# Six depthwise convolution tiles as pairs of positions on TensorE, put right by SBUF transfers

## The chip, the cores and the metric

The kernel runs on one core of a Trainium2 chip. The metric is the device time of one execution, in microseconds; smaller is better. Engines are named as the profile names them: PE is TensorE (PEld its weight loads), DVE is VectorE, ACT is ScalarE, POOL is GpSimd, SP is SyncE, which here only issues DMAs.

## What is computed

The whole trunk of a small diffusion backbone: four layers (RG-LRU, Conformer convolution, neighbourhood attention, RG-LRU), each followed by an MLP, for 128 context and 256 latent tokens of width 1024. The change lies in layer 1, the Conformer module:

```python
def _conformer_conv(h, w_pw1, b_pw1, dw_w, dw_b, ln_g, ln_b, w_pw2, b_pw2):
    val, gate = jnp.split(h @ w_pw1 + b_pw1, 2, axis=-1)
    z = val * jax.nn.sigmoid(gate)
    z = _dwconv_centred(z, dw_w, dw_b)        # 31 taps, each channel by itself
    z = jax.nn.silu(_layernorm(z, ln_g, ln_b))
    return z @ w_pw2 + b_pw2
```

Context and latent tokens are convolved apart, each with zeros beyond its ends. Everything is float32.

## The kernel before

Activations lie with 128 channels on the partitions and the 384 tokens along the free axis, so the 1024 channels are eight tiles, m = 0 to 7. `conformer` goes through them in an order written out by hand. Engines run their own instructions in that order (a scheduler moves some of them within what the data allow), and wait for one another on semaphores.

For each tile `pwin(m)` multiplies by the two column blocks of pw1 (the weights are loaded as `raw` chunks of 1 MB on SP, and split into a high and a low part, `whi` by ACT and `wlo` by DVE), and `glu` makes z from the two products: tanh and a scaled copy on ACT, one product on DVE. z is written into `zp`, a padded row of both token groups with 15 zeros between and around them.

The depthwise convolution is done in two ways. Tiles 0 and 1 (`conv_dve`) take one DVE instruction for each tap over 399 columns. Tiles 2 to 7 go to PE (`conv_mm`): 32 channels at four shifts are the 128 rows of a product, so one product covers four taps, eight steps cover all, and four column groups of 32 channels make up the tile. The rows for that, `z4`, are made by DMA: `zp` goes to DRAM (`zd`), and four DMAs read it back, each with its shift, into 32 partitions. All of these are issued on POOL. The weights `dg`, nearly diagonal blocks made on the host, are loaded on SP. There are three `z4` buffers, so tile m waits for the convolution of tile m-3.

The result of a convolution lies in PSUM with its channels in the right rows. ACT adds the bias for the four tiles in `FIRST`; these four make the mean of LayerNorm first (`shift`: a product with ones gives `mu`, which is taken off so that the sums of squares stay accurate); the later tiles subtract `mu` as they are read. Tile 7 comes last in two segments, the 256 latent columns and then the 128 context columns (`stats`), and is followed at once by the sums of LayerNorm, the normalization (`normed`) and pw2 (products named p). Columns of the modulation matrix for later layers (`pmwl`, products named pmp) are loaded ahead and multiplied behind tile 7.

On PE the order is pw1 of tiles 2 to 5, conv 2, conv 3, pw1 of tiles 6 and 7, conv 4, the mean, conv 5, conv 6, conv 7.

DMAs report their landing on eight semaphores for those issued on SP and ACT (DMAHW0 to 7) and on eight for those issued on POOL (DMASW0 to 7). They are counted off over these in program order; a DMA that shares a semaphore with an earlier one waits until that one has landed.

Of the kernel before, what the change touches and what calls it, by code (L numbers as in the profile page):

```python
# [7 lines left out]
F32 = mybir.dt.float32  # L8
# [3 lines left out]
ALU = mybir.AluOpType  # L12
# [15 lines left out]
CW = 31  # L28
CG = SEQ + 15 + LAT
CSEG = ((0, 0, SEQ), (1, SEQ + 15, CG))  # L30
CP = CG + CW
PE_CONV = (2, 3, 4, 5, 6, 7)
TAP = CW // 4 + 1
ZW = CG + 4 * (TAP - 1)

NH = 16
# [53 lines left out]
LNACT = (1, 3)  # L90
FIRST = (2, 3, 0, 4)
WARM0, WARM1, WARM2 = 20, 8, 4
# [24 lines left out]
@with_exitstack  # L117
def trunk(ctx, tc, wst, wmod, vecs, condr, xin, kcT, vcache, rpbt, diag, ident_in,
          y_out, st_out, k_out, v_out):
# [79 lines left out]
    MODS.clear()  # L199
    loaded = {}  # L200

    def load_chunk(i):
        if plan[i][0] == "gates":
            g = []
            for d in range(2):
                g.append(state["lp"].tile([P, 1024], F32, tag="graw", name=f"graw{i}{d}", bufs=3))
                nc.sync.dma_start(g[d], wst[i, :, d * 1024:d * 1024 + 1024])
            return g
        raw = wp.tile([P, 2048], F32, tag="raw", name=f"raw{i}", bufs=2)
        nc.sync.dma_start(raw, wst[i])  # L210
# [608 lines left out]
    def conformer(l, j, nrm):  # L819
        mv = need(l, G1)  # L820
        with (tc.tile_pool(name=f"cf{l}", bufs=1) as cp,
              tc.tile_pool(name=f"cd{l}", bufs=1, space=bass.MemoryType.DRAM) as dp):
            zps = [cp.tile([P, CP], F32, tag="zp", name=f"zp{l}{i}", bufs=KT) for i in range(KT)]
            for z in zps:
# [3 lines left out]
            def glu(m, pv, pg, c=None):  # L828
                th = tmp(f"gth{l}{m}")[:, :N]
                v = tmp(f"gv{l}{m}")[:, :N]  # L830
                if c is None:
                    nc.scalar.activation(th, pg[:, :N], AF.Tanh, scale=0.5, bias=hb1[:, KT + m:KT + m + 1])
                    nc.scalar.activation(v, pv[:, :N], AF.Identity, scale=0.5, bias=hb1[:, m:m + 1])
# [12 lines left out]
                if m in PE_CONV:  # L846
                    z4 = cp.tile([P, 4, ZW], F32, tag="z4", name=f"z4{l}{m}", bufs=3)
                    zd = dp.tile([P, CP], F32, tag="zd", name=f"zd{l}{m}", bufs=3)
                    nc.gpsimd.dma_start(zd, z)
                    zg = zd.rearrange("(g c) n -> c g n", g=4)  # L850
                    for s in range(4):
                        nc.gpsimd.dma_start(z4[32 * s:32 * s + 32], zg[:, :, s:s + ZW])
                    z4s[m] = z4
                    dgs[m] = wp.tile([P, D], F32, tag="dmw", name=f"dg{l}{m}", bufs=3).rearrange("p (t n) -> p t n", t=TAP)
                    nc.sync.dma_start(dgs[m], diag[PE_CONV.index(m)])

            z4s, dgs, convs = {}, {}, []

# [13 lines left out]

            def conv_pe(m):
                zcs[m] = zc = cp.tile([P, N], F32, name=f"zc{l}{m}")
                ps = conv_mm(m, f"cps{l}{m}", 0, CG)
                for s, a, e in CSEG:
                    _, xa, xb = SEG[s]
                    if m in first:
                        nc.scalar.activation(zc[:, xa:xb], ps[:, a:e], AF.Identity, bias=dwb[:, m:m + 1])
                    else:  # L880
                        nc.vector.scalar_tensor_tensor(zc[:, xa:xb], ps[:, a:e], dwb[:, m:m + 1], mu[:, xa:xb],
                                                       op0=ALU.add, op1=ALU.subtract)
                if m not in first:
                    moments(m)

            def conv_dve(m):
                zcs[m] = zc = cp.tile([P, N], F32, name=f"zc{l}{m}")
                t = cp.tile([P, CG], F32, tag="zt", name=f"zt{l}{m}", bufs=1)
                z = zps[m]
                nc.vector.tensor_scalar(t, z[:, 0:CG], dww[:, m, 0:1], dwb[:, m:m + 1],  # L890
                                        op0=ALU.mult, op1=ALU.add)
                for k in range(1, CW - 1):
                    nc.vector.scalar_tensor_tensor(t, z[:, k:k + CG], dww[:, m, k:k + 1], t,  # L893
                                                   op0=ALU.mult, op1=ALU.add)
                k = CW - 1
                for s, a, e in CSEG:
# [18 lines left out]
            def shift():  # L915
# [3 lines left out]
                for m in first:  # L919
                    center(m)  # L920

            keep = {}
            h = nrm.start([chunk("pw1", j, m) for m in range(2)], f"pw{l}0_",
# [26 lines left out]
            preload(AF.Abs_reciprocal_sqrt, zcs[6][:, 0:1])  # L950
            for i in range(LNPRE):
                t = None
                if i > 3:
                    t = cp.tile([P, 4, ZW], F32, tag="z4", name=f"pmwl{i}", bufs=3)
                    t = t.rearrange("p a b -> p (a b)")[:, :D]
                elif i > 1:
                    t = cp.tile([P, D], F32, tag="pm", name=f"pmwl{i}", bufs=2)
                ready[len(MODS) + i] = mod_load(len(MODS) + i, into=t)
            dl = cp.tile([P, N], F32, name=f"dl{l}")
# [283 lines left out]
def lay_out(i):  # L1243
    import numpy as np
    i = {k: np.asarray(v) for k, v in i.items()}
    chunks = []
    for key in weight_plan():
# [58 lines left out]
    vecs = np.concatenate([bm, cd, sel, lcw, cols(i["lru_conv_b"]), cols(i["lru_b_a"]), cols(i["lru_b_x"]),  # L1306
                           cols(i["lru_lambda"]), cols(i["state_lru"][0]),
                           cols(i["conf_b_pw1"][0].reshape(2, D)), dww, cols(i["conf_dw_b"][0]),
                           cols(i["conf_ln_g"][0]), cols(i["conf_ln_b"][0]), cols(i["conf_b_pw2"][0]),
                           cols(i["final_g"])], axis=1)  # L1310
# [15 lines left out]

    diag = np.zeros((len(PE_CONV), P, TAP, P), f4)
    w = i["conf_dw_w"][0]
    ch = np.arange(32)
    for n, m in enumerate(PE_CONV):  # L1330
        for t in range(TAP):
            for s in range(4):
                if 4 * t + s < CW:
                    for g in range(4):
                        diag[n, 32 * s + ch, t, 32 * g + ch] = w[4 * t + s, m * P + 32 * g + ch]
    ident = np.zeros((P, P), f4)
    ident[np.arange(P), np.arange(P)] = 1
    return dict(wst=wst, wmod=wmod, vecs=vecs, condr=condr, xin=xt, kcT=kcT, vcache=vc, rpbt=rpbt,
                diag=diag, ident_in=ident)

# [29 lines left out]
```

## Time and profile before

| what | value |
|---|---|
| median of 3 runs | 1757.38 us (1752.82 to 1760.23) |
| the profiled execution, its time | 1757.44 us |
| its span in the trace | 1755.7 us |
| TensorE busy | 1725.0 us, 98% |
| mean granted clock | 0.996 |
| the Conformer of layer 1, first product of pw1 to first of pw2 | 456.90 to 575.50 us |

The span runs from the first instruction to the last; the execution's own time is 1.7 us longer. The profile is of that one execution. Times in the trace are from the start of the span. The "chain" follows the work that ended last back to what released it, step by step. In rows of instructions, `out<-in` are the program's names, with the numbers of tiles left out in the profile: `cps` is the convolution's PSUM, `z` is z4, `pw` a product of pw1, `p` one of pw2. A float32 product has two records in the trace, so a tile's 32 products are 64.

### The profile page before, as it was taken

Reading aid. Unit: us, or ns where it says so; the run is one execution under the profiler, and the core shown is the slowest. Engines: PE = TensorE matmul, PEld = TensorE weight load, DVE = VectorE, ACT = ScalarE, POOL = GpSimd, SP = SyncE. Lnnn points to the kernel's source line nnn. Section 1 sums busy time; section 2 is a strip of 40 time slices with the busy share of each in tenths; the row PEclk is TensorE's granted clock in tenths of the full one; section 3 lists DMA queues with packets and bytes.
Section 4 is the critical chain, followed back from the end, with each engine's and each line's share of the span. In section 5 each row is a group of like instructions: output and inputs, shape, how many; then the busy total and the mean of one; then the engine's idle time right before and its main releaser. Section 6 shows DMA issues by size and latency. Waiting matters only on the chain.

```text
span 1755.7 us, 27298 instructions
## 1 busy us (share of the span) xinstructions
PE 1725.0 (98%) x10442; PEld 1626.0 (93%) x10442; DVE 1404.6 (80%) x2791; ACT 946.3 (54%) x1697; POOL 21.6 (1%) x46
## 2 busy tenths in 40 slices
PE   8999999999998999999999999999999999999997
PEld 7779999999985999999987889999999779999997
DVE  5998899999896989889785668889999978843443
ACT  4876662453633774255365657524546976733531
POOL 0000000000021000000000000000000000000000
PEclk9999999999999999999999999999999999999998
DMA  9665367776485247766554423667764413533331
GB/s 387 237 217 179 125 223 255 242 239 237 160 237 170 76 145 251 238 238 232 185 185 160 133 85 132 215 230 236 244 239 167 151 54 121 172 129 120 124 139 39
DMA packets 66996, 322.43 MB, mean 184 GB/s; under 512 B 7952, under 2 KB 12176, under 8 KB 43696
## 3 DMA queue, kind: packets, MB, share of 16 engines
q1 hardware_dynamic: 64944, 314.11, 52.2%
q0 software_dynamic: 1920, 6.57, 1.5%
q8 instruction: 82, 1.34, 0.3%
q14 instruction: 50, 0.41, 0.1%
HBM read 316.69 MB, written 3.96 MB: 183 GB/s over the span
## 4 chain that ended last, share of the span: by engine, by line
PE 77%; DVE 15%; ACT 4%; issue 2%; DMA 1%; SPq 0%; POOL 0%; DVEq 0%; ACTq 0%
PE f L129 29%; PE o L129 27%; PE pw L129 4%; PE lo L129 3%; DVE mjunk L329 3%; PE qk L129 3%; DVE wlo L217 2%; PE p L129 2%; PE wo L129 2%; PE v L129 2%; DVE xf L606 1%; PE cps L129 1%; PE s L129 1%; PE po L129 1%; DVE tr L648 1%
## 5 line engine op out<-in xcount | busy, mean ns | idle before, releaser
L216 ACT ACTIVATE whi<-raw 128x1024 fp32r<-128x1024 f32 x360 | 379.0, 1060 | 545.7 <-PE o L129 326.5
L217 DVE TENSOR_TENSOR wlo<-raw,whi 128x1024 fp32r<-128x1024 f32 x360 | 437.9, 1222 | 161.2 <-ACT whi L216 160.8
L329 DVE SCALAR_TENSOR_TENSOR mjunk<-dmw,condb 128x1024 bf16<-128x1024 f32 x308 | 375.7, 1220 | 1.5
L129 PE MATMUL o<-hl,whi 128*128 128x384 f32 x1024 | 343.0, 335 | 0.0
L129 PE MATMUL o<-hh,wlo 128*128 128x384 f32 x1024 | 343.0, 335 | 0.0
L129 PE MATMUL o<-hh,whi 128*128 128x384 f32 x1024 | 343.0, 335 | 0.0
L129 PEld LDWEIGHTS o<-hh,wlo 128*128 128x128 f32 x1024 | 192.2, 188 | 0.0
L129 PEld LDWEIGHTS o<-hh,whi 128*128 128x128 f32 x1024 | 192.2, 188 | 0.0
L129 PEld LDWEIGHTS o<-hl,whi 128*128 128x128 f32 x1024 | 192.2, 188 | 0.0
L499 DVE SCALAR_TENSOR_TENSOR x<-o,modv,x 128x128 f32<-128x128 f32 (+1 forms) x128 | 47.4, 413 | 68.2 <-PE o L129 68.2
L129 PE MATMUL g<-xf,graw 128*128 128x386 f32 x256 | 85.7, 490 | 1.8 <-DVE gl L664 1.8
L129 PEld LDWEIGHTS g<-xf,graw 128*128 128x128 f32 x256 | 47.9, 190 | 34.4 <-DVE gl L664 2.5
L783 DVE TENSOR_TENSOR hl<-s,hh 128x384 fp32r<-128x384 f32 x128 | 71.2, 556 | 7.4 <-ACT s L782 3.1
L781 ACT ACTIVATE hh<-r 128x384 fp32r<-128x384 f32 x128 | 67.2, 525 | 3.3
L782 ACT ACTIVATE s<-r 128x384 f32<-128x384 f32 x128 | 65.3, 511 | 0.0
L777 ACT ACTIVATE r<-f 128x384 f32<-128x384 f32 x112 | 52.9, 473 | 12.2 <-PE f L129 12.2
L129 PE MATMUL lo<-yh,wlo 128*128 128x384 f32 x128 | 43.5, 340 | 1.6 <-DVE wlo L217 1.6
L129 PE MATMUL lo<-yl,whi 128*128 128x384 f32 x128 | 43.0, 336 | 0.0
L129 PE MATMUL lo<-yh,whi 128*128 128x384 f32 x128 | 42.6, 336 | 0.0
L129 PE MATMUL cps<-z,dg 128*32 128x399 f32 (+2 forms) x448 | 34.7, 467 | 4.5 <-DMA z<-zd 4.5
L893 DVE SCALAR_TENSOR_TENSOR zt<-zp,vec,zt 128x399 f32<-128x399 f32 x58 | 36.7, 632 | 1.2
L129 PEld LDWEIGHTS cps<-z,dg 128*32 128x32 f32 x448 | 14.6, 114 | 23.8 <-issue 22.4
(1515 smaller groups left out, 4030.4 us busy)
## 6 DMA issues: line engine op xcount, KB each, us to landing
raw<-wst SPq DMA_DIRECT2D x180, 1024.0 KB, 5.0
dmw<-wmod SPq DMA_DIRECT2D x154, 512.0 KB, 4.1
pmw<-wmod SPq DMA_DIRECT2D x34, 512.0 KB, 7.3
graw<-wst SPq DMA_DIRECT2D x16, 512.0 KB, 5.1
bt<-rpbt SPq DMA_DIRECT2D x16, 384.0 KB, 3.3
z<-zd POOLq DMA_DIRECT2D x24, 213.5 KB, 6.3
dg<-diag SPq DMA_DIRECT2D x6, 512.0 KB, 4.8
pmwl<-wmod SPq DMA_DIRECT2D x4, 512.0 KB, 5.4
```

The costliest lines, as they stand in the source:

```text
L129: i = nc.tensor.matmul(*a, **kw)
L216: nc.scalar.activation(hi, raw[:, s], AF.Copy)
L217: nc.vector.tensor_tensor(lo, raw[:, s], hi.bitcast(F32), op=ALU.subtract)
L329: nc.vector.scalar_tensor_tensor(mjunk, w, 0.5, condb[:, s], op0=ALU.mult, op1=ALU.mult, accum_out=mod_tile(l)[:, c, m, s:s + 1]))
L499: nc.vector.scalar_tensor_tensor(x[m][:, xa:xb], ps[:, a:b], mv[:, g, m, s:s + 1], x[m][:, xa:xb], op0=ALU.mult, op1=ALU.add)
L606: nc.vector.scalar_tensor_tensor(xf, r[:, k:k + LG], lcw[:, j, t, k:k + 1], xf, op0=ALU.mult, op1=ALU.add)
L648: nc.vector.tensor_tensor_scan(tr[:, 2 + mt, ::-1], a[:, 2 + mt, ::-1], ti[:, 2 + mt, ::-1], h0v[:, j, 1, t:t + 1], op0=ALU.mult, op1=ALU.add)
L777: nc.scalar.activation(r, ps[:, :N], AF.Relu)
L781: nc.scalar.activation(hh, r, AF.Square)
L782: nc.scalar.activation(s, r, AF.Square)
L783: nc.vector.tensor_tensor(hl, s, hh.bitcast(F32), op=ALU.subtract)
L893: nc.vector.scalar_tensor_tensor(t, z[:, k:k + CG], dww[:, m, k:k + 1], t, op0=ALU.mult, op1=ALU.add)
```

## The change

- Tiles 1 to 6 are convolved by `conv_pair`. A product's 128 rows are 16 channels by 8 successive inputs, and its 32 columns are 16 channels by two neighbouring positions; four steps cover the taps, and with 200 pairs of positions one product has 200 columns. Eight groups of 16 channels by four steps make 32 products for a tile. Tile 0 alone stays on DVE. Tile 7 is as before.
- z is written into `zp` with even and odd positions apart. `z4` is filled by eight DMAs of 16 partitions. Tiles 1 to 4 issue theirs on POOL, tiles 5, 6 and 7 on SP (`SYNCZ`).
- In PSUM a row now holds one parity of the positions of a channel. ACT copies PSUM to `co` in SBUF, and four DMAs of 64 partitions from SBUF to SBUF, issued on ACT, put channels and positions right in `zq`. The channel order within a tile that comes out of that is taken up by the host, in the rows of pw2, the bias and the LayerNorm's vectors (`turn`). `conv_in` then does from `zq` what was done from PSUM: bias on ACT for tiles 0 to 3, bias and `mu` on DVE for tiles 4 to 6.
- The order on PE becomes pw1 of tiles 2 to 4, conv 1, conv 2, pw1 of 5, conv 3, pw1 of 6, three products of the mean, pw1 of 7 with the mean's fourth product in it, conv 4, conv 5, conv 6, conv 7. `FIRST` is tiles 0 to 3.
- The loads of pmwl are split in two (`lnload`): three ahead of pw1 of tile 6, three at the end, in buffers of z4. `ensure` loads one weight chunk further ahead at two places.

What this does to three queues. On POOL, where the convolutions begin (`zd` is the copy to DRAM of one tile, `z4` the DMAs back; the number after the 1 of the layer is the tile). Before:

```order
L849 DMA zd12_4971<-zp12_4647 128x430
L852 DMA z412_4970<-zd12_4971 32x4x427 x4
L849 DMA zd13_5080<-zp13_4648 128x430
L852 DMA z413_5079<-zd13_5080 32x4x427 x4
L849 DMA zd14_5155<-zp14_4649 128x430
L849 DMA zd15_5230<-zp15_4650 128x430
L852 DMA z414_5154<-zd14_5155 32x4x427 x4
```

and after:

```order
L866 DMA zd11_4901<-zp11_4646 128x432
L866 DMA zd12_4984<-zp12_4647 128x432
L877 DMA z411_4900<-zd11_4901 16x8x212 x8
L877 DMA z412_4983<-zd12_4984 16x8x212 x8
L866 DMA zd13_5097<-zp13_4648 128x432
L866 DMA zd14_5176<-zp14_4649 128x432
```

Tile 1 is new on the queue; the copies of two tiles stand together, and each tile's reading back is eight DMAs.

On SP, at the end of the convolutions (`dg` convolution weights, `raw` weights of pw2). Before:

```order
L855 DMA dg15_5236<-diag 128x1024 [waits DMAHW2_49,PE_49]
L855 DMA dg16_5417<-diag 128x1024 [waits DMAHW3_49,PE_49]
L210 DMA raw58_5932<-wst 128x2048 [waits DMAHW0_49,DVE_49]
L210 DMA raw59_6094<-wst 128x2048 [waits DMAHW1_49,DVE_49]
L855 DMA dg17_5492<-diag 128x1024 [waits PE_49]
L165 DMA pmwl4_5665<-wmod 128x1024 [waits DMASW2_49,DMASW3_49,DMASW1_49,DMASW4_49,DMASW0_49,PE_49]
```

and after, from the fourth DMA of z4 of tile 6 on:

```order
L877 DMA z416_5475<-zd16_5476 16x8x212 [waits DMAHW5_49]
L877 DMA z416_5475<-zd16_5476 16x8x212 [waits DMAHW7_49]
L877 DMA z416_5475<-zd16_5476 16x8x212 [waits DMAHW0_49]
L877 DMA z416_5475<-zd16_5476 16x8x212 [waits DMAHW1_49]
L877 DMA z416_5475<-zd16_5476 16x8x212 [waits DMAHW2_49]
L866 DMA zd17_5583<-zp17_4652 128x432 [waits DMAHW3_49,DVE_49,Pool_49]
L872 DMA dg17_5584<-diag 128x1024 [waits DMAHW4_49,PE_49]
L218 DMA raw59_6170<-wst 128x2048 [waits DMAHW5_49,Activation_49]
L870 DMA z417_5582<-zd17_5583 32x4x428 [waits DMASW5_49,DMASW6_49,DMASW4_49,DMASW7_49,DMASW3_49,DMAHW3_49,DMASW2_49,DMAHW6_49,DMASW1_49,DMASW0_49]
L870 DMA z417_5582<-zd17_5583 32x4x428 [waits DMAHW1_49]
L870 DMA z417_5582<-zd17_5583 32x4x428 [waits DMAHW4_49]
L870 DMA z417_5582<-zd17_5583 32x4x428 [waits DMAHW5_49]
```

The transfers of tiles 6 and 7 now stand on SP in one line with dg7 and raw59. The semaphores DMAHW0 to 7 are shared with the transfers on ACT that are shown next, and counting them off gives who waits for whom. Of tile 6 the fourth, fifth and sixth transfers wait for the first, third and fourth of zq of tile 4, and the eighth for the first of zq of tile 5. zd7 waits for the second of zq of tile 5, dg7 for the third. raw59 waits for the fourth transfer of tile 6. Of tile 7 the first waits for zd7 and for the fourth of zq of tile 5, the third for dg7, and the fourth for raw59.

On ACT, at conv 4 and conv 5. Before:

```order
L832 ACTIVATE gth17_5479<-pw17_1_5454,hb1_219 128x384 [waits PE_49]
L833 ACTIVATE gv17_5480<-pw17_0_5429,hb1_219 128x384
L879 ACTIVATE zc14_5494<-cps14_5495,vec_70 128x128 [waits PE_49]
L879 ACTIVATE zc14_5494<-cps14_5495,vec_70 128x256
L918 ACTIVATE mu1_4661<-mu1p_4662 128x384 [waits PE_49]
L357 ACTIVATE va1q0_5536<-zc12_5238 128x384 [waits DVE_49]
```

and after:

```order
L842 ACTIVATE gv17_5577<-pw17_0_5526,hb1_219 128x384
L224 ACTIVATE whi58_0_6010<-raw58_6008 128x1024 [waits DMAHW2_49]
L912 ACTIVATE co14_5624<-cps14_5591 128x400 [waits PE_49]
L915 DMA zq14_5625<-co14_5624 64x200 [waits DMAHW5_49,Activation_49]
L915 DMA zq14_5625<-co14_5624 64x200 [waits DMAHW6_49]
L915 DMA zq14_5625<-co14_5624 64x200 [waits DMAHW7_49]
L915 DMA zq14_5625<-co14_5624 64x200 [waits DMAHW0_49]
L912 ACTIVATE co15_5664<-cps15_5631 128x400 [waits PE_49]
L915 DMA zq15_5665<-co15_5664 64x200 [waits Activation_49]
L915 DMA zq15_5665<-co15_5664 64x200 [waits DMAHW3_49]
L915 DMA zq15_5665<-co15_5664 64x200 [waits DMAHW4_49]
L915 DMA zq15_5665<-co15_5664 64x200 [waits DMAHW6_49]
```

The reading of PSUM with the bias has become a copy and four DMAs.

The diff, cut to its core:

```diff
-PE_CONV = (2, 3, 4, 5, 6, 7)
+PAIR_CONV = (1, 2, 3, 4, 5, 6)
+LAST = 7
+SYNCZ = (5, 6, 7)
-FIRST = (2, 3, 0, 4)
+FIRST = (0, 1, 2, 3)
...
                 for s, a, b in SEG:
-                    o = 15 + 15 * s
-                    nc.vector.scalar_tensor_tensor(z[:, a + o:b + o], th[:, a:b], 1.0, v[:, a:b],
-                                                   op0=ALU.add, op1=ALU.mult)
-                if m in PE_CONV:
+                    o = 15 + CGAP * s
+                    dst, p, q = z[:, a + o:b + o], th[:, a:b], v[:, a:b]
+                    if m in PAIR_CONV:
+                        o = a // 2 + 8 * s
+                        dst = z[:, 7:7 + 2 * PV + 2].rearrange("p (f v) -> p f v", f=2)[:, :, o:o + (b - a) // 2]
+                        p, q = (t.rearrange("p (v f) -> p f v", f=2) for t in (p, q))
+                    i = nc.vector.scalar_tensor_tensor(dst, p, 1.0, q, op0=ALU.add, op1=ALU.mult)
+                dma = (nc.sync if m in SYNCZ else nc.gpsimd).dma_start
+                if m == LAST or m in PAIR_CONV:
...
+                    dma(zd, z[:, :CP])
...
+                        zg = zd[:, :2 * PV].rearrange("(g c) (f v) -> c g f v", g=8, f=2)
+                        for t in range(8):
+                            i = dma(z4[16 * t:16 * t + 16], zg[:, :, 1 - t % 2, t // 2:t // 2 + PZ])
+                        dg = dg.rearrange("p (k g n) -> p k g n", k=4, g=8)
+                        nc.sync.dma_start(dg, pairw[PAIR_CONV.index(m)])
...
+            def conv_pair(m):
+                ps = mm_tile(f"cps{l}{m}")[:, :CG].rearrange("p (r u) -> p r u", r=2)
+                for r in range(2):
+                    for k in range(4):
+                        for g in range(4):
+                            i = matmul(ps[32 * g:32 * g + 32, r], dgs[m][:, k, 2 * g + r],
+                                       z4s[m][:, 2 * g + r, 4 * k:4 * k + CU], start=k == 0, stop=k == 3)
+                convs.append(i.ins)
+                o = cp.tile([P, 2, CU], F32, tag="co", name=f"co{l}{m}", bufs=2)
+                zq = cp.tile([P, 2, CU], F32, tag="zq", name=f"zq{l}{m}", bufs=2)
+                nc.scalar.activation(o, ps, AF.Copy)
+                for r in range(2):
+                    for f in range(2):
+                        evs[m] = nc.scalar.dma_start(zq[r:P:2, f], o[f:P:2, r]).ins
+                zqs[m] = zq
+
+            def conv_in(m):
...
+                    src = zqs[m][:, :, a // 2:e // 2]
...
             pwin(4)
+            conv_pair(1)
+            conv_pair(2)
+            with tc.issue_after(evs[2]):
+                conv_in(1)
             pwin(5)
-            conv_pe(2)
-            conv_dve(1)
-            conv_pe(3)
+            conv_pair(3)
+            with tc.issue_after(gvs[-1]):
+                conv_in(2)
+            lnload(0, 3)
+            ensure(state["w"] + 3)
             pwin(6)
+            with tc.issue_after(gvs[-1]):
+                conv_in(3)
+            ensure(state["w"] + 3)
+            last, (hi, lo) = state["pe"], copied[state["w"]]
+            with tc.issue_after(last), tc.issue_after(hi), tc.issue_after(lo):
+                shift()
             pwin(7)
-            conv_pe(4)
-            shift()
-            conv_pe(5)
-            center(1)
-            conv_pe(6)
+            conv_pair(4)
+            conv_pair(5)
+            with tc.issue_after(evs[5]):
+                conv_in(4)
+            preload(AF.Abs_reciprocal_sqrt, zcs[4][:, 0:1])
+            conv_pair(6)
+            with tc.issue_after(evs[6]):
+                conv_in(5)
+                conv_in(6)
...
+            lnload(3, LNPRE)
```

More of the change, by code (lines that the diff above doesn't have):

```diff
@@ L28 @@
 CW = 31
-CG = SEQ + 15 + LAT
-CSEG = ((0, 0, SEQ), (1, SEQ + 15, CG))
-CP = CG + CW
-PE_CONV = (2, 3, 4, 5, 6, 7)
+CGAP = 16
+CG = SEQ + CGAP + LAT
+CSEG = ((0, 0, SEQ), (1, SEQ + CGAP, CG))
+CP = CG + CW + 1
+PAIR_CONV = (1, 2, 3, 4, 5, 6)
+LAST = 7
 TAP = CW // 4 + 1
+SYNCZ = (5, 6, 7)
 ZW = CG + 4 * (TAP - 1)
+CU = CG // 2
+PV = CU + 15
+PZ = CU + 12
+ZB = 2 * (PV + 1) + 8
 NH = 16
@@ L822, in conformer @@
               tc.tile_pool(name=f"cd{l}", bufs=1, space=bass.MemoryType.DRAM) as dp):
-            zps = [cp.tile([P, CP], F32, tag="zp", name=f"zp{l}{i}", bufs=KT) for i in range(KT)]
+            zps = [cp.tile([P, ZB], F32, tag="zp", name=f"zp{l}{i}", bufs=KT) for i in range(KT)]
             for z in zps:
@@ L851, in glu @@
[L851 to L857, printed above, removed]
+                    dg = wp.tile([P, D], F32, tag="dmw", name=f"dg{l}{m}", bufs=3)
+                    dma(zd, z[:, :CP])
@@ new lines, in glu @@
+                    if m == LAST:
+                        zg = zd.rearrange("(g c) n -> c g n", g=4)
+                        for s in range(4):
+                            i = dma(z4[32 * s:32 * s + 32], zg[:, :, s:s + ZW])
+                        dg = dg.rearrange("p (t n) -> p t n", t=TAP)
+                        nc.sync.dma_start(dg, diag)
+                    else:
+                        z4 = z4.rearrange("p a b -> p (a b)")[:, :8 * PZ].rearrange("p (g v) -> p g v", g=8)
+                        zg = zd[:, :2 * PV].rearrange("(g c) (f v) -> c g f v", g=8, f=2)
[3 more added lines that the diff above has]
+                        nc.sync.dma_start(dg, pairw[PAIR_CONV.index(m)])
@@ L920, in shift, with lnload @@
                     center(m)
+            def lnload(a, b):
+                for i in range(a, b):
+                    t = None
+                    if i > 2:
+                        t = cp.tile([P, 4, ZW], F32, tag="z4", name=f"pmwl{i}", bufs=3)
+                        t = t.rearrange("p a b -> p (a b)")[:, :D]
+                    elif i > 1:
+                        t = cp.tile([P, D], F32, name=f"pmwl{i}")
+                    ready[len(MODS) + i] = mod_load(len(MODS) + i, into=t)
             keep = {}
@@ L949, in conformer @@
                     nc.scalar.activation(x[m][:, a:b], x[m][:, a:b], AF.Identity, bias=gb[:, m, s:s + 1])
[L950 to L958, printed above, removed]
+            lnload(3, LNPRE)
             dl = cp.tile([P, N], F32, name=f"dl{l}")
@@ L1245, in lay_out @@
     i = {k: np.asarray(v) for k, v in i.items()}
+    turn = np.arange(D).reshape(KT, P)
+    for m in PAIR_CONV:
+        turn[m] = turn[m].reshape(4, 2, 16).transpose(0, 2, 1).reshape(P)
+    turn = turn.reshape(D)
     chunks = []
@@ L1325, in lay_out @@
     rpbt = bt.reshape(KT, 2, 2, P, N).transpose(0, 3, 1, 2, 4)
-    diag = np.zeros((len(PE_CONV), P, TAP, P), f4)
     w = i["conf_dw_w"][0]
+    diag = np.zeros((P, TAP, P), f4)
     ch = np.arange(32)
[L1330 to L1335, printed above, removed]
+    for t in range(TAP):
+        for s in range(4):
+            if 4 * t + s < CW:
+                for g in range(4):
+                    diag[32 * s + ch, t, 32 * g + ch] = w[4 * t + s, LAST * P + 32 * g + ch]
+    pairw = np.zeros((len(PAIR_CONV), P, 4, 8, 32), f4)
+    ch = np.arange(16)
+    for n, m in enumerate(PAIR_CONV):
+        for k in range(4):
+            for t in range(8):
+                for f in range(2):
+                    if 0 <= 8 * k + t - f < CW:
+                        for g in range(8):
+                            pairw[n, 16 * t + ch, k, g, 2 * ch + f] = w[8 * k + t - f, m * P + 16 * g + ch]
     ident = np.zeros((P, P), f4)
```

52 lines of the change are left out of this document (31 added, 21 removed).

## The prediction

> **What bounds the kernel now.** First the page: its first line, and the busy shares below it.
>
> ```profile
> span 1755.7 us, 27298 instructions
> PE 1725.0 (98%) x10442; PEld 1626.0 (93%) x10442; DVE 1404.6 (80%) x2791; ACT 946.3 (54%) x1697; POOL 21.6 (1%) x46
> ```
>
> TensorE is busy 98% of the span, so a saving counts only where it shortens TensorE's row of work without opening a gap in it. The change lies in one stage, the Conformer of layer 1. I read the chain of work that ended last, over that stage (start, duration, what):
>
> ```profile
> 507.50 10.87 PE cps L129 x112
> 518.36 16.87 PE pw L129 x96
> 535.23 5.50 PE cps L129 x61
> 540.73 2.79 PE mu1p L129 x8
> 543.52 4.98 issue
> 548.50 1.64 POOL z L852 x3
> 550.13 8.51 DMA z<-zd
> 558.64 0.25 issue
> 558.88 5.32 PE cps L129 x64
> ...
> 575.50 2.58 PE p L129 x8
> ```
>
> Up to 543.52 TensorE sets the pace: tiles 2 and 3 (10.87), pw6 and pw7 (16.87), tile 4 (5.50), the mean (2.79). Then the chain leaves TensorE: z of tile 7 is issued at 548.50 and its last transfer takes 8.51 us, while tiles 5 and 6 run beside it. Then comes tile 7 at 558.88, the LayerNorm, and the next matrix at 575.50. The waits of TensorE in the stage (total, times, longest) say what that costs:
>
> ```profile
> PE cps L129 <- DMA z<-zd: 4.5, 1, 4.5
> PE p L129 <- ACT yh L405: 2.7, 1, 2.7
> ```
>
> So the stage ends with a transfer, not with a product: what tile 7 waits for decides, and products made shorter ahead of 558.88 are worth nothing by themselves. The clock behind both gaps, in stretches of TensorE (from:to, length, busy, granted clock, DMA share, GB/s):
>
> ```profile
> 554.40:558.90 4.50, 0.02 (x3) 1.00 1.03 259
> 558.90:562.20 3.30, 3.30 (x32) 0.50 0.37 151
> 562.20:564.20 2.00, 2.00 (x37) 0.98 0.03 8
> 576.00:579.40 3.40, 3.40 (x13) 0.51 0.00 0
> ```
>
> A gap thus also costs about half of 3.3 us, 1.65 us, at half clock. [...]
>
> **The change: the products.** Prices of one tile by shape (busy, mean ns of one):
>
> ```profile
> L129 PE MATMUL cps<-z,dg 128*32 128x399 f32 x320 | 27.4, 498 | 0.0
> L129 PE MATMUL cps<-z,dg 128*32 128x128 f32 x64 | 2.0, 274 | 0.0
> ```
>
> A tile of 399 columns is 64 records and 27.4/5 = 5.48 us; 64 records of 128 columns took 2.0. For 64 records of 200 columns I interpolate: 2.0 + 72/271 x 3.48 = 2.9 us (bounds 2.0 and 5.48). Ahead of the end of conv4 stand two such tiles and tile 4 before (16.4 us), four pair tiles after (tile 1 is new; 11.6). The mean stays. So the end of conv4 with the mean behind it, 543.52, becomes T = 538.7 if nothing stalls.
>
> **Its transfers ahead.** POOL's own row (start, duration, idle before), and what one issue and one landing cost (minimum, median, maximum), for z and then for zd:
>
> ```profile
> 485.11 0.69 POOL L849 DMA_DIRECT2D zd<-zp  x1 [24.88 <-DVE zt L893]
> 487.94 2.19 POOL L852 DMA_DIRECT2D z<-zd  x4 [2.13 <-DMA zd<-zp]
> L852 POOL DMA_DIRECT2D z<-zd x24: 552/552/569, 487.9 to 550.1; - x24
> DMA to landing us min/median/max: 3.4/6.3/8.5
> L849 POOL DMA_DIRECT2D zd<-zp x6: 559/563/695, 485.1 to 541.2; - x6
> DMA to landing us min/median/max: 2.5/4.1/7.2
> ```
>
> Tile 1 needs z now, and every z is eight transfers instead of four. From about 487, when zd1 has landed, the eighth of z1 is issued at 487 + 7 x 0.55 = 490.9. Each transfer of z2 waits for the one of z1 with its number, since they share a completion semaphore. The DMA engines are full there:
>
> ```profile
> 490.00:492.00 2.00, 0.12 (x1) 1.00 0.98 399
> 494.00:496.00 2.00, 0.56 (x1) 1.00 1.08 223
> ```
>
> So I take 7 us a landing, between median and maximum: z1 there at 497.9, z2 at 504.9. TensorE ends pw4 at 499.0 (507.50 less one matrix tile of 16.87/2), conv1 at 501.9, and waits 3.0 us (0 by the minimum, 6.0 by the maximum) and then 1.65 at half clock. T = 543.4, bounds 538.7 and 546.4. z3 follows z2 by one more landing, about 511 to 516.5, before conv3 at about 518, behind pw5: hidden.
>
> **The end: what tile 7 waits for.** After the change, SP and ACT count their DMAs off on the same eight semaphores, and each DMA waits until the earlier one on its semaphore has landed. By the order, z6 has transfers behind those of zq4 and zq5; zd7 waits for the second transfer of zq5, dg7 for the third, raw59 stands behind dg7, and z7's fourth transfer waits for raw59 to land. zp7, ready soon after pw7, is no longer what z7 waits for. The prices (landings of dg, of raw, of 64 KB from SBUF and of 64 KB to it, in that order; the first row is the issue on SP, the last an ACT copy out of PSUM):
>
> ```profile
> L855 SPq DMA_DIRECT2D dg<-diag x6: 327/328/328, 437.4 to 540.8; - x6
> DMA to landing us min/median/max: 3.5/4.8/7.2
> DMA to landing us min/median/max: 4.7/5.0/12.9
> DMA to landing us min/median/max: 1.5/1.7/2.3
> DMA to landing us min/median/max: 3.0/3.8/5.4
> 536.05 0.56 ACT L832 ACTIVATE gth<-pw,hb 128x384 f32<-128x384 f32 x1
> ```
>
> From T: conv5 2.9; the copy to co 0.6; the third zq transfer issued 0.7 later and landed 2.0 after that (no SBUF to SBUF transfer is in the trace; 1.5 to 3.8 by the 64 KB rows, nearest the first of them); dg7's issue 0.33 and the wake 0.2; raw59 landed 5.0 later (4.7; up to 9.9, about halfway to its maximum); the last z7 3.4 (the minimum, since few others then run; up to 8.5); the wake of TensorE 0.25. Sum 15.4, so tile 7 starts at 543.4 + 15.4 = 558.8; before 558.9. conv6 fits in: its last z6 waits for the first of zq5, so it starts near T + 9.5 and ends about T + 13 with part of it at half clock.
>
> [...]
>
> **What costs nothing.** Thirty steps of tile 1 leave VectorE:
>
> ```profile
> L893 DVE SCALAR_TENSOR_TENSOR zt<-zp,vec,zt 128x399 f32<-128x399 f32 x58 | 36.7, 632 | 1.2
> ```
>
> That is 30 x 0.63 = 19 us of VectorE; zp7 comes earlier, but zd7 waits for zq5, so I count 0. ACT gets 24 issues (24 x 0.33 = 8 us) and six copies (3.4 us), and loses six evictions' reads of PSUM; over 520 to 540 it has room (busy 6.22 of 20):
>
> ```profile
> 520.00:540.00 20.00, 6.22 (x9) 1.00 0.64 170
> ```
>
> If that cover goes, the copy of conv5 is late, and its delay goes one for one into the last sum. The split of the LayerNorm's loads and the checks on loaded weights move transfers that TensorE reaches after 558.9: 0, as long as pmwl5, now behind conv7's first segment, lands in 5 us or so.
>
> Behind tile 7 the LayerNorm and the 16.62 us to 575.50 stay. The gap before tile 7 shrinks from 4.5 us to some 2, so between 0 and 1.65 us of half clock go: 0.8.
>
> **The sum**, against the profiled execution: -0.1 from tile 7's start, -0.8 of clock, so 0.9 less than a time that is at the median to a tenth: 1756.5 us. By the lower ends (T 538.7, then 14.4; clock -1.65) tile 7 starts at 553.1, and 1750 comes out; by the upper ones together (T 546.4, then 27) 573.4, 1772.
>
> **Rivals.**
> *The gain arrives.* If the shared semaphores hold nothing up, z7 goes from zp7: pw7 ends at T - 2.9, zp7 2 us on, zd7 4.1, z7 1.6 of issue and 6.3: T + 11.1. With no stall at conv2 that is 549.8, and 1747.5. For it: VectorE is free, and pw7's end is all zp7 needs. Against it: the waits stand in the program, the DMA share was 1.03 in the gap, and with the stall at conv2 the same way gives 1752.
>
> *Contention makes the end later: slower.* The chain zq, raw59, z7 is three landings in a row, and a full DMA system stretches each. At the share of 1.03 (554 to 559) the last z7 took 8.51. With landings of 3.0, 9.9 and 8.5 tile 7 comes 24 to 26 us behind T, with T at 543 to 546 at 568 to 572; 1770. It decides from a start later than 567.7, 8.8 us behind today's. For it: raw at 12.9 and z at 8.5 were seen. Against it: after 543 few loads but raw59 are left.
>
> *The products are not shorter.* If a product of 32 columns of weights is bound by its issue, a pair tile takes 5.48: T comes 10 us later, the end too: 1767. Against it: 64 records of 128 columns took 2.0.
>
> **How the numbers follow.** About 0.5%, 8.8 us, is what a measurement of this kernel can tell from no change. The gain arrives 0.12 (all of its terms at their good ends); contention 0.14; the products not shorter 0.03; the forecast 0.71, with its own range 1750 to 1765. Of the forecast's cases hardly any leave the 0.5%. Slower takes 0.17, faster 0.12. Range 1749.5 to 1767: 1 in 10 outside on each side.
>
> **What would show it.** Right: records of 200 columns at some 330 to 380 ns, a pair tile at about 2.9 us; a wait of 0 to 6 us at conv2 for z; conv6 and conv7 waiting for z, with z7's last transfer issued only once raw59 has landed; tile 7 starting between 553 and 567; zq landing near 2 us. Wrong: no wait ahead of conv6, or z7 issued within 5 us of pw7's end (then the gain arrives); conv4 held by z4; ACT's copies late behind weight copies, or mean and LayerNorm waiting for zq; idle time of TensorE after 575 that was not there.

## The result, and the profile after

The changed kernel took 1770.71 us (median of 4; 1769.06 to 1773.51), the kernel before 1755.76 beside it (median of 4). The ratio is 1.0068 with a 95% interval of 1.0046 to 1.0090: slower by some 12 to 15 us. The forecast was 1756.5 within 1749.5 to 1767; the time lies 4 us above the range, near the time that the rival of contention had named (1770). Medians and ratios here and below are of undisturbed runs; one run of conv_behind_pw5 (3447.09 us) is left out of its row.

The first lines of the page of after, span and busy shares:

```profile
span 1768.0 us, 27496 instructions
PE 1722.5 (97%) x10506; PEld 1632.9 (92%) x10506; DVE 1386.8 (78%) x2760; ACT 947.9 (54%) x1703; POOL 24.3 (1%) x52
```

TensorE's busy time fell by 2.5 us only (1725.0 before), and the span rose by 12.3, so TensorE waits more. Its waits in the stage of the Conformer (total, times, longest):

```profile
PE cps L136 <- DMA z<-zd: 19.6, 3, 7.3
PE p L136 <- ACT yh L414: 2.7, 1, 2.7
PE cps L136 <- DMA zq<-co: 1.2, 1, 1.2
```

One wait of 4.5 us for z has become three of 19.6. The products of the convolution show where (start, duration, what; the idle time before it in brackets):

```profile
498.45 2.92 PE L136 MATMUL cps<-z,dg 128*32 128x200 f32 x64
508.16 5.38 PE L136 MATMUL cps<-z,dg 128*32 128x200 f32 x64 [6.80 <-DMA z<-zd]
523.23 2.92 PE L136 MATMUL cps<-z,dg 128*32 128x200 f32 x64 [1.15 <-DMA zq<-co]
545.80 5.62 PE L136 MATMUL cps<-z,dg 128*32 128x200 f32 x128
558.74 5.56 PE L136 MATMUL cps<-z,dg 128*32 128x200 f32 x64 [7.32 <-DMA z<-zd]
```

A pair tile takes 2.92 us, as forecast (2.9, against 5.48 before). But conv2 starts 6.8 us late and runs mostly at half clock (5.38), conv3 waits 1.15 us, and so conv4 (the first half of the fourth row) ends at 548.76; in the kernel before, conv4 and the mean behind it were done at 543.52. conv6 waits 7.3 us more and again runs at half clock. The profile puts conv3's wait down to zq of tile 2. z of tile 3 came at the same moment: POOL's last issue for tile 4, which waits for tile 3's last transfer, went at 523.11. Then the chain, from z of tile 1 to pw2:

```profile
486.35 3.69 POOL z L877 x7
490.03 8.32 DMA z<-zd
...
498.64 9.43 DMA z<-zd
...
508.16 5.43 PE cps L136 x64
...
545.87 2.89 PE cps L136 x64
...
556.66 9.81 DMA raw<-wst
...
566.49 3.04 DMA z<-zd
...
569.78 6.05 PE cps L136 x64
...
587.07 1.91 PE p L136 x8
```

Two landings of z, 8.32 and 9.43 us, stand in a row before conv2. At the end raw59 takes 9.81 us, and only then does the last transfer of z7 go. Tile 7 starts at 569.78 instead of 558.88 (10.9 us later), pw2 at 587.07 instead of 575.50 (11.6). All but 0.7 us of the 12.3 are lost by the end of this stage.

How full the DMA engines were in this stretch says more. The software queue, which is POOL's, from 480 to 530 (packets, MB, the time of its packets as a share of 16 engines), first of before:

```profile
q0 software_dynamic: 1280, 4.38, 36.9%
```

and of after:

```profile
q0 software_dynamic: 1788, 4.36, 46.6%
```

The same 4.4 MB (z, and with it zd, a fifth of the bytes) cost 295 us of engine time before (0.369 x 16 x 50 us) and 373 after: 14.8 and 11.7 GB/s an engine. Bytes of z became dearer, and tile 1 adds a seventh tile on TensorE with its own z, zd and weights.

### The profile page after: what moved, and what is told of

It is laid out like the page before. It is cut to its first block, busy times and chain, and to the rows that moved or that the text cites. A ratio compares the mean times of both kernels' runs of the same rounds, so it can differ in the third digit from the quotient of the medians.

```text
span 1768.0 us, 27496 instructions
## 1 busy us (share of the span) xinstructions
PE 1722.5 (97%) x10506; PEld 1632.9 (92%) x10506; DVE 1386.8 (78%) x2760; ACT 947.9 (54%) x1703; POOL 24.3 (1%) x52
## 4 chain that ended last, share of the span: by engine, by line
PE 74%; DVE 15%; ACT 4%; DMA 4%; issue 2%; SPq 0%; POOL 0%; ACTq 0%; DVEq 0%
PE f L136 29%; PE o L136 26%; PE lo L136 3%; DVE mjunk L338 3%; PE qk L136 3%; DVE wlo L225 2%; PE p L136 2%; PE wo L136 2%; PE pw L136 2%; PE v L136 1%; DMA z<-zd 1%; DVE xf L615 1%; PE cps L136 1%; DMA raw<-wst 1%; PE s L136 1%
## 5 line engine op out<-in xcount | busy, mean ns | idle before, releaser
L136 PE MATMUL cps<-z,dg 128*32 128x200 f32 (+2 forms) x512 | 30.4, 405 | 20.8 <-DMA z<-zd 19.6
L136 PEld LDWEIGHTS cps<-z,dg 128*32 128x32 f32 x512 | 20.6, 132 | 30.1 <-issue 23.7
L136 PE MATMUL wo<-oT,whi 128*128 128x384 f32 x128 | 33.7, 343 | 0.0
```

The lines of the kernel that those rows point to most:

```text
L136: i = nc.tensor.matmul(*a, **kw)
```

## The experiments

Times are compared by ratio to runs of the kernel before on the same chip, whose medians lay between 1755.8 and 1760.5. "conv4" is the end of conv4, "tile 7" the start of its product, both in the profiled execution.

| kernel | median | ratio to before (95%) | conv4 | tile 7 |
|---|---|---|---|---|
| before | 1755.76 | 1 | 540.7 | 558.9 |
| after | 1770.71 | 1.0068 (1.0046 to 1.0090) | 548.8 | 569.8 |
| z7_pool | 1772.42 | 1.0076 (1.0061 to 1.0091) | 549.7 | 568.3 |
| z_all_pool | 1773.06 | 1.0078 (1.0063 to 1.0093) | 549.2 | 571.5 |
| conv_behind_pw5 | 1772.31 | 1.0076 (1.0059 to 1.0093) | 554.5 | 573.8 |
| no_zq | 1763.89 | 1.0040 (1.0025 to 1.0056) | 550.0 | 563.0 |
| long_rows | 1772.72 | 1.0084 (1.0063 to 1.0104) | 553.2 | 572.2 |
| z_half | 1756.77 | 1.0002 (0.9988 to 1.0016) | 539.1 | 555.9 |
| raw_half | 1766.51 | 1.0046 (1.0027 to 1.0064) | 546.1 | 565.1 |
| spread | 1765.25 | 1.0039 (1.0024 to 1.0053) | 545.9 | 568.1 |
| two_copies | 1771.09 | 1.0076 (1.0053 to 1.0099) | 551.3 | 572.0 |
| before_spread | 1751.77 | 0.9961 (0.9946 to 0.9976) | 540.3 | 554.1 |
| before_spread_again | 1751.20 | 0.9951 (0.9938 to 0.9963) | 540.4 | 554.1 |
| spread4 | 1755.69 | 0.9982 (0.9969 to 0.9996) | 541.8 | 557.8 |
| spread4_pool | 1755.12 | 0.9975 (0.9965 to 0.9985) | 542.1 | 557.5 |
| spread4_zqp | 1750.99 | 0.9950 (0.9931 to 0.9969) | 540.3 | 552.7 |
| spread4_late59 | 1754.44 | 0.9968 (0.9956 to 0.9980) | 540.4 | 552.3 |

(In the two kernels of the old layout the mean, 2.8 us, comes behind conv4, in the others ahead of it. In the two runs of before_spread, tile 7's start is the end of the mean and two tiles of 5.48.)

### Undoing the order, one piece at a time

My first theory was that of the prediction: order and shared semaphores. Its rival was that the DMA system is full and the order only passes the wait on.

```diff
-SYNCZ = (5, 6, 7)
+SYNCZ = (5, 6)
```

> Only tile 7's zd and z go back to POOL's queue (SYNCZ = (5, 6)). Theory A (shared completion semaphores put zq5, dg7 and raw59 in front of z7): z7 leaves soon after zp7, about 551 to 553, and is there before conv6 ends, so conv7 follows conv6 near 564 with no gap and no half clock: about 7 us less than the changed kernel, 1763. Theory B (only the bytes in the full DMA system count, the order does not): z7 shares the engines with raw59 and lands when it did, about 566 to 569: 0 to 3 us less, 1768 to 1771.

```diff
-SYNCZ = (5, 6, 7)
+SYNCZ = ()
```

> All z and zd on POOL (SYNCZ empty), zq stays on ACT. Theory A: z6 no longer waits for zq5, so conv6 follows conv5 without the 7.3 us wait, and conv7 starts when z7 has landed, near 559: 10 us or so less than the changed kernel, 1760. The stall at conv2 stays. Theory B: 0 to 3 us less, and the 0.53 us of POOL's issue instead of SP's 0.33 takes some of it back.

```diff
+            pwin(5)
             conv_pair(1)
             conv_pair(2)
             with tc.issue_after(evs[2]):
                 conv_in(1)
-            pwin(5)
             conv_pair(3)
```

> Tiles 1 and 2 are convolved behind pw1 of tile 5 instead of ahead of it; nothing else. If the early stall is only that conv2 is asked for before its transfers can be there (z2 landed at 508, pw5 ends near 507), the 6.8 us wait, the 2.5 us of half clock and the 1.15 us before conv3 go, and the end keeps its own waits: about 10 us less than the changed kernel, 1760. Theory B (the DMA system stays full and the wait only moves on to conv3 or conv4): 3 us less or nothing.

All three came out with the rival: 1.0076 to 1.0078, none faster than after. The waits of TensorE in z7_pool:

```profile
PE cps L136 <- DMA z<-zd: 19.9, 3, 11.2
PE lnm L136 <- DVE me1a L379: 6.8, 1, 6.8
```

Tile 7 now waits for nothing, but z6 lands later (conv6 waits 11.2 us instead of 7.3), its zq is late in turn, and the LayerNorm waits 6.8 us for the sums. In z_all_pool conv6 still waits, 9.6 us. In conv_behind_pw5 the stall at conv2 is gone and stands before conv3:

```profile
PE cps L136 <- DMA z<-zd: 24.8, 3, 13.4
```

So undoing the order alone only moved the wait from one tile to another, as if all z transfers queued for something that they share.

### Leaving out zq

```diff
-                zq = cp.tile([P, 2, CU], F32, tag="zq", name=f"zq{l}{m}", bufs=2)
-                nc.scalar.activation(o, ps, AF.Copy)
-                for r in range(2):
-                    for f in range(2):
-                        evs[m] = nc.scalar.dma_start(zq[r:P:2, f], o[f:P:2, r]).ins
-                zqs[m] = zq
+                evs[m] = nc.scalar.activation(o, ps, AF.Copy).ins
+                zqs[m] = o
```

> The four SBUF to SBUF transfers of each tile are left out and the bias is added from co, so positions and channels are not put right (the output is not the reference's). ACT's 24 DMA issues and the places of zq on the shared semaphores go. Theory A: z6, zd7 and dg7 wait for nothing late and z7 no longer for raw59; conv6 follows conv5 and conv7 starts near 557: 12 us or so less than the changed kernel, 1758, with the stall at conv2 unchanged. Theory B: 1.2 MB fewer of some 25 MB in the stage, 1 to 3 us less.

It gained 0.28 points of ratio (some 5 us), less than half of the 12 expected. conv6 did follow conv5, but z7 then needed 8 us to land, and the early stalls stayed. So zq, with its bytes, its issues on ACT and its places on the semaphores, stands for 0.28 of the 0.68 points, and does not explain the early stalls.

### Bytes, rows, or the count of transfers

```diff
-                            i = dma(z4[16 * t:16 * t + 16], zg[:, :, 1 - t % 2, t // 2:t // 2 + PZ])
+                            i = dma(z4[16 * t:16 * t + 16, :4], zg[:, :4, 1 - t % 2, t // 2:t // 2 + PZ])
...
-                                       z4s[m][:, 2 * g + r, 4 * k:4 * k + CU], start=k == 0, stop=k == 3)
+                                       z4s[m][:, (2 * g + r) % 4, 4 * k:4 * k + CU], start=k == 0, stop=k == 3)
```

> Each DMA of z of tiles 1 to 6 brings four of its eight groups of channels (the products of the other four read the same rows again, so the output is not the reference's); transfers, queues and semaphores are as in the changed kernel. Theory C: half of z's engine time goes, conv3 near 515, 8 to 12 us less than the changed kernel. Theory D: conv3 stays near 523, the time within 2 us of 1770.

```diff
-        nc.sync.dma_start(raw, wst[i])
+        half = 52 <= i < 60
+        nc.sync.dma_start(raw[:, :1024] if half else raw, wst[i, :, :1024] if half else wst[i])
...
-            s = slice(h * 1024, h * 1024 + 1024)
+            s = slice(0, 1024) if half else slice(h * 1024, h * 1024 + 1024)
```

> The weight chunks of pw1 of tiles 2 to 7 and the first two of pw2 are loaded by half (their second half repeats the first, so the output is not the reference's); count and order of transfers stay. Theory C: 6 x 1.5 us of engine time less before 523 and raw59 landing in half its 9.8 us: conv3 near 514, conv7 some 15 us earlier, 1755. Theory D with raw59 alone at fault: conv3 stays near 523, raw59 and so conv7 5 us earlier, 1765.

z_half gave the whole loss back (1.0002), with the count of transfers unchanged: conv1 and conv2 ran without a gap, conv3 started at 513.6, and conv4 ended at 539.1, where the prediction's sum without a stall had put it (538.7). The waits:

```profile
PE cps L136 <- DMA z<-zd: 11.3, 1, 11.3
PE p L136 <- ACT yh L414: 2.7, 1, 2.7
PE cps L136 <- DMA zq<-co: 0.8, 1, 0.8
```

raw_half took half of 8 MB of weights out of the stage, and gained only 0.22 points: raw59 landed in 6.7 us, conv2 still waited 4.8, and 1766.51 is near the 1765 of theory D. The software queue from 480 to 530, of z_half and of raw_half:

```profile
q0 software_dynamic: 1280, 2.62, 20.4%
```

```profile
q0 software_dynamic: 1792, 4.36, 48.5%
```

In raw_half that is 11.2 GB/s an engine, no more than the 11.7 of after, so the weights' share is not what makes z slow. In z_half it is 16.1: with half of z in flight each byte cost less, too.

```diff
...
+                        for f in range(2):
+                            dma(zg[:, f].rearrange("c (g v) -> g c v", g=8), z[:, f * PV:f * PV + PV])
                         for t in range(8):
-                            i = dma(z4[16 * t:16 * t + 16], zg[:, :, 1 - t % 2, t // 2:t // 2 + PZ])
+                            i = dma(z4[16 * t:16 * t + 16, :8 * PV - 3], zg[:, 1 - t % 2, t // 2:t // 2 + 8 * PV - 3])
...
```

> The same bytes of z in long rows: zd of a pair tile is written as 16 rows of 8 channels by 215 positions for each parity (two DMAs of 860 byte rows), so each of the eight DMAs back reads 16 rows of 6868 bytes instead of 128 of 848; order, queues and the count of z transfers stay. Theory C (the DMA engines' time is what runs out from 490 to 526: the short rows of z moved at 10.7 GB/s an engine where 8 KB rows moved at 21.7): some 2.5 us less for each tile's z, conv3 near 515 instead of 523, z6 and z7 sooner too: 8 to 12 us less than the changed kernel, 1759 to 1763. Theory D (the number of transfers and their order on shared semaphores, each with its latency): conv3 stays near 523, and the time within 2 us of 1770.

A miss for theory C in this form: 1.0084, and the software queue hardly cheaper:

```profile
q0 software_dynamic: 1597, 4.18, 44.1%
```

That is 11.8 GB/s an engine with rows of 6868 bytes, 11.7 with rows of 848. The length of a row is not it.

### Source or destination

```diff
-                            i = dma(z4[16 * t:16 * t + 16], zg[:, :, 1 - t % 2, t // 2:t // 2 + PZ])
+                            i = dma(z4[t:P:8], zg[:, :, 1 - t % 2, t // 2:t // 2 + PZ])
...
-                            pairw[n, 16 * t + ch, k, g, 2 * ch + f] = w[8 * k + t - f, m * P + 16 * g + ch]
+                            pairw[n, 8 * ch + t, k, g, 2 * ch + f] = w[8 * k + t - f, m * P + 16 * g + ch]
```

> The changed kernel with one number changed in z's transfers of tiles 1 to 6: the 16 rows of a transfer go to every eighth partition of z4 instead of 16 neighbouring ones (the host lays the weights' rows to match). Bytes, rows, order and semaphores stay. While z runs nearly alone the trace shows the engines full at some 140 GB/s. Theory E (the destination: 16 neighbouring partitions take bytes slowly): z as fast as in z_half, conv3 near 514, 10 to 14 us less than the changed kernel, 1757 to 1761. Theory G (the source: eight reads of one 216 KB copy in DRAM): no change, 1768 to 1773.

```diff
+                        ze = dp.tile([P, CP], F32, tag="ze", name=f"ze{l}{m}", bufs=3)
+                        dma(ze, z[:, :CP])
                         for t in range(8):
+                            zg = (ze if t % 2 else zd)[:, :2 * PV].rearrange("(g c) (f v) -> c g f v", g=8, f=2)
```

> The changed kernel with a second copy of each pair tile in DRAM (one more DMA of 216 KB a tile); the odd shifts are read from it. Theory G (reads of one small region are slow): z faster in spite of it, conv3 5 us or more sooner, 1762 to 1766. Theory E (the destination): no gain and some 0.6 us of engine time more a tile: 1770 to 1776.

```diff
-                        nc.gpsimd.dma_start(z4[32 * s:32 * s + 32], zg[:, :, s:s + ZW])
+                        nc.gpsimd.dma_start(z4[s:P:4], zg[:, :, s:s + ZW])
...
-                        diag[n, 32 * s + ch, t, 32 * g + ch] = w[4 * t + s, m * P + 32 * g + ch]
+                        diag[n, 4 * ch + s, t, 32 * g + ch] = w[4 * t + s, m * P + 32 * g + ch]
```

> The kernel before, with each z transfer's 32 rows sent to every fourth partition instead of 32 neighbouring ones (weights' rows to match); nothing else. Theory E: the 4.5 us wait for z of tile 7 shrinks (its last transfer took 8.51 us): 2 to 6 us less than before, with the half clock behind it. Theory G: within 2 us of before.

The destination it is. A second copy to read from gained nothing (1.0076). Rows sent to every eighth partition took the ratio from 1.0068 to 1.0039; the two intervals just touch, but beside two_copies on the same chip every run of spread was faster (1761.62 to 1767.66 against 1770.80 to 1776.38). That is about 5 us, half or less of the 10 to 14 expected: conv2 still waited 2.8 us, conv3 started at 520.4 and not near 514, and tile 7, whose rows were not spread, still waited 6.9. The same kind of edit to the kernel before, with 32 rows to every fourth partition, made that kernel faster than it was: 0.9961, some 7 us where 2 to 6 were expected. The software queue from 480 to 530, of spread:

```profile
q0 software_dynamic: 1792, 4.36, 36.2%
```

and of before_spread:

```profile
q0 software_dynamic: 1280, 4.38, 22.7%
```

In GB/s an engine, for the same 4.4 MB: 11.7 into 16 neighbouring partitions, 15.1 into 16 partitions eight apart, 14.8 into 32 neighbouring ones, 24.1 into 32 partitions four apart. As above, a fifth of these bytes is zd. In before_spread TensorE waits for no z at all: its chain runs through tiles 5 and 6 and the first segment of tile 7 in one piece, and of the waits those before the LayerNorm's sums and pw2 are left:

```profile
543.14 14.32 PE cps L129 x175
```

```profile
PE p L129 <- ACT yh L405: 2.7, 1, 2.7
PE lnm L129 <- DVE zc L973: 0.2, 1, 0.2
```

That the numbers of the partitions alone change the rate is measured: 16 rows went from 11.7 to 15.1 when they were laid eight apart, 32 rows from 14.8 to 24.1 when they were laid four apart. What in the hardware makes it so, no run here tells.

### The change with that cured

```diff
-                        for t in range(8):
-                            i = dma(z4[16 * t:16 * t + 16], zg[:, :, 1 - t % 2, t // 2:t // 2 + PZ])
+                        zg = zd.rearrange("p n -> (p n)").rearrange("(g c v) -> c g v", g=8, v=PV)
+                        for k in range(4):
+                            i = dma(z4[k:P:4], zg[:, :, k:k + PZ])
...
-                            i = dma(z4[32 * s:32 * s + 32], zg[:, :, s:s + ZW])
+                            i = dma(z4[s:P:4], zg[:, :, s:s + ZW])
...
```

> The changed kernel with z laid out so that one transfer brings both parities of a shift: four DMAs of 32 rows of 8 x 848 bytes a tile instead of eight of 16, each to every fourth partition of z4, tile 7's too (weights' rows to match). Queues and order stay, so zq, dg7 and raw59 still share semaphores with z7. Theory E: z at 20 GB/s an engine or more, no wait at conv2 and conv3, the end of conv4 near 540; if the semaphores at the end then decide, conv7 starts near 556 as in z_half: 1751 to 1757. If they do not, conv7 follows conv6 near 547: 1743 to 1748.

```diff
-                        evs[m] = nc.scalar.dma_start(zq[r:P:2, f], o[f:P:2, r]).ins
+                        evs[m] = (nc.scalar if m < 4 else nc.gpsimd).dma_start(zq[r:P:2, f], o[f:P:2, r]).ins
```

> spread4 with the transfers of zq of tiles 4 to 6 issued on POOL, which counts them off on its own semaphores; z7 then waits for nothing but zd7. Theory A for the end: conv7 follows conv6 near 547, 6 to 10 us less than spread4. If bytes decide there: within 2 us of spread4.

```diff
-SYNCZ = (5, 6, 7)
+SYNCZ = ()
```

> spread4 with all z and zd on POOL (SYNCZ empty) and zq on ACT. Theory A for the end: as spread4_zqp, 1743 to 1750, with POOL's 0.55 us an issue against SP's 0.33. If bytes decide: within 2 us of spread4.

spread4 gives the whole loss back: 0.9982, 15 us below after in the medians and a little below before. The stall at conv2 is gone (conv1 and conv2 run in one piece, conv4 ends at 541.8); a wait of 1.2 us before conv3 and one ahead of tile 7 remain:

```profile
PE cps L136 <- DMA z<-zd: 10.7, 1, 10.7
PE cps L136 <- DMA zq<-co: 1.2, 1, 1.2
```

The software queue from 480 to 530:

```profile
q0 software_dynamic: 1536, 4.36, 25.0%
```

That is 21.8 GB/s an engine into 32 partitions four apart, with rows of 848 bytes. spread4 also halves the count of z transfers and spreads tile 7's, so no run tells which of these is worth how much of the step from spread (1.0039) to 0.9982.

At the end the shared semaphores now stand alone. SP's own waits from 540 to 556 (dg7 is L873, z7 is L871):

```profile
SPq L871 <- DMA dg<-diag: 3.2, 1, 3.2
SPq L873 <- DMA zq<-co: 3.1, 1, 3.1
SPq L871 <- DMA zq<-co: 3.0, 1, 3.0
```

dg7 waits for a transfer of zq, z7's second transfer for dg7, and its third for the last zq of tile 5. raw59, issued at 545.99, holds nothing up here, though the prediction had it in this chain. From that last zq on, the chain is:

```profile
547.38 6.55 DMA zq<-co
...
554.57 3.02 DMA z<-zd
...
557.84 5.23 PE cps L136 x64
```

With zq on POOL's own semaphores the wait falls to 7.0, and the ratio to 0.9950:

```profile
PE cps L136 <- DMA z<-zd: 8.6, 2, 7.0
PE lnm L136 <- DVE me1a L379: 1.8, 1, 1.8
```

0.32 points, some 5 us, a little less than the 6 to 10 expected: the shared semaphores do cost time, once z is quick. (The edit also takes the issuing off ACT, whose copy of conv5 came 2 us sooner, at 543.06; no run has the one without the other.) conv7 does not follow conv6: z7, now issued from 543.13 on, took 7.6 us to land. spread4_pool, which takes z and not zq off them, gained 0.07 points, within its interval nothing. POOL issued its z7 at 548.26, 5 us later than SP in spread4_zqp, behind a zd7 that took 5.2 us to land. Theory A for the end holds for zq and not for that way round.

```diff
-        nc.sync.dma_start(raw, wst[i])
+        if i == 59 and "z7" in state:
+            with tc.issue_after(state["z7"]):
+                nc.sync.dma_start(raw, wst[i])
+        else:
+            nc.sync.dma_start(raw, wst[i])
...
```

> spread4_zqp with raw59's load issued behind z7's last transfer instead of ahead of its first. If raw59 takes z7's engine time (z7 landed in 7.6 us there): z7 lands in 4 to 5 us, conv7 starts 2 to 4 us sooner, 1747 to 1749, unless zq6, whose sums came 1.8 us late already, then decides: 1750. If zd7's path decides: within 1 us of spread4_zqp.

> The kernel before with its z rows spread over every fourth partition, run again beside spread4_late59: 1750 to 1753, as in its first run. The pair products are worth something over it only if spread4_late59 is 2 us or more below.

Loading raw59 behind z7 did not help: 0.9968 against 0.9950, the intervals overlapping. z7 landed in 6.1 us instead of 7.6 but left 1 us later, and the LayerNorm then waited for zq of tile 6:

```profile
PE lnm L136 <- DVE me1a L383: 2.6, 1, 2.6
```

before_spread repeated its time: 1751.20, ratio 0.9951 (0.9938 to 0.9963). So the fastest version with pair products (0.9950) and the kernel before with two lines changed (0.9961 and 0.9951) cannot be told apart; both are some 0.4 to 0.5% below before.

## Why the prediction was wrong

- **Which stage and what bounds it.** Right: the 11.6 us by which pw2 comes later lie between the first convolution and pw2, and transfers set the stage's end.
- **The products.** Right: 2.92 us a pair tile against 2.9, and without a stall conv4 at 539.1 (z_half) against 538.7.
- **The stall at conv2.** The step that failed first. The place was right, the size not: I took 7 us a landing and got a wait of 3.0 with 1.65 of half clock; z landed in 8.32 and 9.43, the wait was 6.8, and conv2 took 5.38 instead of 2.92, 2.5 more. Also conv3, which I had called hidden, waited 1.15. End of conv4: 548.8 against T = 543.4, above my upper bound of 546.4. Behind it stands the real error: I priced the new z transfers by the landings of the old ones, whose rows went to 32 partitions. The prediction itself printed the rows that should have warned: before moved 399 GB/s at a DMA share of 0.98 and, four microseconds on, 223 at 1.08. I read "full" as "many bytes". In before, in a stretch in which only the software queue moved bytes (length, POOL's busy time, clock, DMA share, GB/s):

```profile
518.00:520.00 2.00, 0.38 (x1) 1.00 1.02 222
```

  and in after, in a stretch in which z was nearly all that moved:

```profile
514.00:516.00 2.00, 2.00 (x5) 1.00 1.09 140
```

- **The end.** The order of waits was right: conv6 behind z6's last transfer, then dg7 and raw59 on SP, and z7's last transfer behind raw59 (issued at 566.49, when raw59 had landed). The size was not: 21.0 us from conv4's end to tile 7, against 15.4. raw59 was issued 1.2 us later than in the sum, and took 9.81 where I took 5.0; that term alone is 4.8 of the 5.6. The 5.0 was the median landing of the whole run. That few others run then, my reason for z7's 3.4, held for z7's last transfer (3.04) and not for raw59, beside which dg7 and three z7 transfers ran. With z spread, raw59 landed in 7.0 (spread4, spread4_zqp); why not in 5.0 stays open.
- **Contention as a rival.** It had the mechanism for raw59 (9.9 against 9.81) and nearly the time (1770), at a chance of 0.14. The time is partly luck: it took 24 to 26 us from conv4's end, with z7's last at 8.5, and got 21.0 with 3.04, while conv4 ended 2.8 us or more later than it had. Its evidence against, that only raw59 is left after 543, was wrong, as above. That a quick z cures the whole loss (z_half, spread4) shows that slow transfers were the cause; that the partitions made them slow stood in no rival.
- **What costs nothing.** VectorE's 19 us were worth nothing on the path, as forecast: before_spread has tile 1 on VectorE and is as fast as the best pair version.
- **The clock.** I weighed it at 0.8 in the kernel's favour, for a gap of some 2 us before tile 7. The rows that I had read show half clock behind gaps of 4.5 and 2.7 us and have none of 2, so the 0.8 was my estimate and no run shows it. It went the other way: conv2, conv6 and tile 7 each began at half clock, which lasted 4.9 us or more and not 3.3, and behind a gap of 5.5 us tile 7's first segment took 6.05 us against 5.32 before.
- **Another issuer.** Moving z from SP to POOL gave no gain (1.0076 and 1.0078 against the 1.0068 of after, and 0.9975 against the 0.9982 of spread4). Moving zq from ACT to POOL did gain (0.9950 against 0.9982): z7 no longer waited for zq, and TensorE's wait for z7 fell from 10.7 to 7.0 us.

## What to carry to other kernels

When a change makes a transfer of another shape, price it by the engine time that a byte takes into that many partitions at those numbers (here 11.7 to 24.1 GB/s an engine), not by the landing of the old one. Here a DMA share of 1.08 with 223 GB/s beside one of 0.98 with 399 meant that the transfers were slow, and not that there were many; moving them between queues only moved the wait (1.0076 and 1.0078), while spreading the rows over the partitions (in the kernel before one slice, `z4[s:P:4]` for `z4[32 * s:32 * s + 32]`, and the host's weights to match) removed it (no wait for z in before_spread, 0.9961). And halve the suspect's bytes before building on a chain of semaphores: the chain was real, but undoing it gained nothing while z was slow, and some 5 us once the 15 of z had been won back.

## What the runs showed of the hardware

- The rate of z into SBUF went with the numbers of the partitions, at equal bytes: 11.7 GB/s an engine into 16 neighbours (after), 14.8 into 32 neighbours (before), 15.1 into 16 eight apart (spread), 24.1 and 21.8 into 32 four apart (before_spread, spread4), z and zd together. The length of the rows (848 or 6868 bytes) made 11.7 into 11.8. It is not the partitions alone: half the bytes into the same 16 partitions moved at 16.1 (z_half).
- Transfers from SBUF to SBUF of 50 KB (64 rows of 800 bytes to every second partition) landed in 1.7 us at best, 3.3 at the median and 12.4 at worst, in after; the forecast had 2.0.
- Half clock followed idle gaps of 6.8, 7.3 and 5.5 us in after, and lasted 5.1 us of work in conv2, all 5.56 us of conv6 and 4.9 us in tile 7; before, it lasted about 3.4 us there (558.88 to 562.30), behind a gap of 4.5. The gap of 1.15 us before conv3 was followed by full clock (2.92). In stretches of after (length, busy, granted clock, DMA share, GB/s):

```profile
508.20:513.00 4.80, 4.80 (x60) 0.50 0.83 269
...
558.80:564.20 5.40, 5.40 (x64) 0.50 1.04 338
...
569.80:574.50 4.70, 4.70 (x48) 0.50 0.96 374
```

- The prediction counted 1.65 us of half clock behind its wait of 3.0 us at conv2, as before has it behind gaps of 4.5 and 2.7 us. The gap of 2.72 us before pw2 does not always cost it. The same kernel in its two runs, before_spread first and before_spread_again below it:

```profile
568.80:571.00 2.20, 2.20 (x7) 0.52 0.00 0
```

```profile
568.80:571.00 2.20, 2.18 (x13) 1.00 0.00 0
```
